# Neighbourhood attention by pairs of heads, with products alternating between halves of the systolic array

## The chip, the cores and the metric

The kernel runs on one NeuronCore of a Trainium2 chip as a single launch. The metric is the device time of one execution in microseconds, lower is better. The engines are named as in the profile: PE (TensorE, matrix products; PEld is its weight load), DVE (VectorE), ACT (ScalarE), POOL (GpSimd) and SP (SyncE, which issues most DMAs). [...]

## What is computed

The reference is a two-layer backbone over 256 latent tokens and 256 context tokens of width 1024. The mixer of layer 0 joins neighbourhood attention (8 heads of dimension 64) with a Hyena operator. The change touches only that attention. Each latent query sees a window of the grid and all context keys in one softmax; context queries see the context keys.

```python
def neighbourhood_attention(q, k, v, k_ctx, v_ctx, rpb):
    ...
        s_win = jnp.einsum('bhqd,bhrqjd->bhqrj', q_r, k_w).astype(jnp.float32) * scale + bias
        s_ctx = jnp.einsum('bhqd,bhcd->bhqc', q_r, k_ctx).astype(jnp.float32) * scale
        s = jnp.concatenate([s_win.reshape(b, h, GRID_W, n_win), s_ctx], axis=-1)
        p = jax.nn.softmax(s, axis=-1).astype(v.dtype)
        p_win = p[..., :n_win].reshape(b, h, GRID_W, wr, WIN_C)
        return (jnp.einsum('bhqrj,bhrqjd->bhqd', p_win, v_w)
                + jnp.einsum('bhqc,bhcd->bhqd', p[..., n_win:], v_ctx))

def dense_attention(q, k, v):
    s = jnp.einsum('bhqd,bhkd->bhqk', q, k).astype(jnp.float32) * (q.shape[-1] ** -0.5)
    p = jax.nn.softmax(s, axis=-1).astype(v.dtype)
    return jnp.einsum('bhqk,bhkd->bhqd', p, v)

# layer 0: na_hyena_mixer
    a_lat = merge_heads(neighbourhood_attention(qk_norm(qa_l, q_gain), qk_norm(ka_l, k_gain), va_l,
                                                k_c, va_c, rpb))
    b_lat = hyena_operator(p_lat[..., 3 * NA_WIDTH:], conv_w, conv_b, filter_params, d_bias)
    o_lat = jnp.concatenate([a_lat, b_lat], axis=-1) @ w_out
    ...
    a_ctx = merge_heads(dense_attention(qk_norm(qa_c, q_gain), k_c, va_c))
```

## The kernel before

All activations lie feature-major in SBUF: 128 features on the partitions, 512 tokens (256 latent, 256 context) along the free axis. Most products keep float32 accuracy by splitting each operand into a high and a low part (names ending in hi and lo) and taking three products hi·hi, lo·hi, hi·lo. The program's order is written out by hand: each engine's queue has its instructions in the order in which the Python code emits them. A tile of the PSUM pool psp (seven banks) or of the page pool in SBUF is reused once its last reader is done.

The attention (mixer0, line 911) runs beside the Hyena projections in a loop of 12 steps. Step i first makes one projection tile: in_tile (line 563), 24 products of 512 columns into the tile pi. It fetches its weight with w_get, which also splits a later weight tile (ACT writes whi, DVE writes wlo, line 153) and, in its place, issues the DMA of another from SP. Then attend(i) (line 1075) does one step of the attention: the values of head i-2, the transposes of head i-1, and the scores of head i. After it come the two halves of a Hyena convolution (conv; DVE lines 918 and 920; tiles x1c in even steps, vc in odd ones), with the head's exponentials (exps, on ACT) between them and its normalising (norm, on DVE) behind them. In some steps the transposes pzt of a Hyena block (z_trans) follow.

For one head, the pieces are:

- scores (line 992): queries and keys of two heads share a tile pair, head 2b on partitions 0 to 63 and head 2b+1 on partitions 64 to 127. A product has a 64-row contraction. psc holds the scores of 128 latent queries against all 512 keys (two tiles per head), pscc those of 2 x 128 context queries against 256 context keys. DVE then takes maxima (lines 1013 to 1019), adding the position bias, a tile loaded per head by load_bias from SP.
- exps and norm: ACT exponentiates into pr and prc and sums into sm; DVE inverts sm (line 1033) and scales pr and prc (lines 1035, 1037).
- transposes (line 1042): 12 PE transposes into ptp and ptc, copied to pt and ptc in SBUF by ACT and DVE (line 1051).
- values (line 1063): six products with a 64-column result into one half of the partitions of pao, in plain float32, which PE runs as two passes each. When both heads of a pair are done, cat_put splits pao into chi and clo (line 181).

The inner loop of the score products, which the change rewrites, is

```python
            def mm(o, q0, k0):
                for n, (a, b) in enumerate(((q, k), (q, kl), (ql, k))):
                    T.matmul(o, lhsT=a[r, q0:q0 + P], rhs=b[r, k0:], start=n == 0, stop=n == 2)
```

where r is the head's half of the partitions. In the opening stage of the kernel (mods, line 789) there are products of another small shape: their results have 32 rows, and successive products go to the four groups of 32 partitions of the tile pmod in turn.

Of the kernel before, what the change touches and what calls it, by code (L numbers as in the profile page):

```python
# [30 lines left out]
# columns of the packed per-partition constants  # L31
# [18 lines left out]
def _mod_tiles():  # L50
    """(layer, index, feature block) of the modulation VectorE makes, in order."""
    return [(l, i, b) for l, i in [(0, j) for j in range(2, 9)] + [(1, j) for j in range(9)] for b in range(KB)]


def body(ctx, tc, I, out):
# [38 lines left out]
    # ---------------------------------------------------------------- constants  # L94
# [11 lines left out]
    # ---------------------------------------------------------------- weights  # L106
# [52 lines left out]
    def w_halves():  # L159
        """The next tile's split in two steps; nothing is loaded in its place."""  # L160
# [22 lines left out]
    def w_paged():  # L183
        """The next tile, split into pages: for where whl's buffers are all in use."""
# [27 lines left out]
    # ---------------------------------------------------------------- modulation  # L212
# [37 lines left out]
    # ---------------------------------------------------------------- residual and norms  # L250
# [8 lines left out]
    def sumsq(s, m, late=None):  # L259
        """Adds block m's squares; the addition itself is left to the caller where a list is given."""  # L260
# [16 lines left out]
    def rsqrt_steps(y, src, scale, n):  # L277
        """y (SBUF) = (src*scale + eps)^-1/2, src in PSUM; one VectorE operation between yields."""
# [25 lines left out]
    def norm_h(s, k, l, n, dst):  # L304
        """dst: (hi, lo) APs of block k, stream s. Returns what is left to do once hi is there."""
# [25 lines left out]
    # H: list of KB (hi, lo), each [P, 512] = lat | ctx  # L331
# [15 lines left out]
    class Norm:  # L347
        """Norm n of layer l, whose sums of squares are complete per stream in turn."""
# [117 lines left out]
    def first_group(norm, mid=None):  # L466
        """The first 4 feature tiles after a norm; the latents go first, the context's norm runs beside."""
# [102 lines left out]
    # ---------------------------------------------------------------- SwiGLU  # L570
# [62 lines left out]
    def parted(a, j):  # L633
        """a[j] becomes its two parts."""
# [79 lines left out]
    def decay_scalars():  # L714
        """Decay exponents: log_sigmoid of the logits."""
# [20 lines left out]
    def start():  # L736
# [78 lines left out]
        def normed(s, m):  # L815
            """Blocks 2m and 2m+1 of stream s, normed."""
# [93 lines left out]
    # ---------------------------------------------------------------- layer 0 mixer  # L910
    def mixer0(norm_in, norm_out):
# [62 lines left out]
        # attention  # L974
# [9 lines left out]
        def qk_split(b):  # L984
            """Queries and keys of heads 2b and 2b + 1 in two parts each."""
# [6 lines left out]
        def scores(h):  # L992
            r = slice(64 * (h % 2), 64 * (h % 2) + 64)
            (q, ql), (k, kl) = qks[h // 2]
            bi = bias.pop(h)

            def mm(o, q0, k0):
                for n, (a, b) in enumerate(((q, k), (q, kl), (ql, k))):
                    T.matmul(o, lhsT=a[r, q0:q0 + P], rhs=b[r, k0:], start=n == 0, stop=n == 2)
# [3 lines left out]
            for qb in range(2):  # L1003
                mm(pl[qb], qb * P, 0)
# [546 lines left out]
```

## Time and profile before

| | |
|---|---|
| median of 3 timed runs | 1912.69 us (1911.32 to 1914.88) |
| the profiled execution, its span | 1918.3 us |
| PE busy | 1894.8 us (99%) |
| DVE busy | 1210.1 us (63%) |
| ACT busy | 701.5 us (37%) |
| POOL busy | 65.6 us (3%) |
| mean granted TensorE clock | 0.994 of full speed |

The profiled execution is one run recorded by the hardware profiler; its span reaches from the first to the last instruction. [...] A release shown in brackets names what ended an idle time.

### The profile page before, as it was taken

The numbers are of one execution on the slowest core, as the hardware profiler recorded it, in microseconds if no ns is written. First come the engines' busy times: TensorE is split into PE (matmuls) and PEld (weight loads), VectorE is DVE, ScalarE is ACT, GpSimd is POOL, SyncE is SP. The second block draws the span as 40 slices with busy tenths as digits, with TensorE's granted clock in tenths as the row PEclk, the third lists the DMA queues.
The fourth block names the chain that finished last, engine by engine and source line by source line (L and its number), as shares of the span: only waits on it lengthen the run. The fifth ranks groups of instructions, "written<-read, shape, count | busy, mean of one in ns | idle before, by whom it ended". The sixth has DMA issues, their size and how long they took to land.

```text
span 1918.3 us, 26355 instructions
## 1 busy us (share of the span) xinstructions
PE 1894.8 (99%) x10646; PEld 1627.5 (85%) x10646; DVE 1210.1 (63%) x1870; ACT 701.5 (37%) x1085; POOL 65.6 (3%) x73
## 2 busy tenths in 40 slices
PE   8999999999999999999999999999999999999999
PEld 5788888798877798878887988888889999999999
DVE  5577677777676776676766655433346755567554
ACT  4332122245554352222222422122233544465442
POOL 1010000002001200000000000000000200000000
PEclk9999999999999999999999999999999999999999
DMA  9355445532323235554555256423323432355653
GB/s 355 117 175 197 150 165 183 200 95 82 99 66 92 77 108 166 174 197 144 185 193 169 85 190 209 142 88 94 116 82 99 133 100 88 100 178 184 197 181 129
DMA packets 77899, 277.52 MB, mean 145 GB/s; under 512 B 8657, under 2 KB 9681, under 8 KB 77650
## 3 DMA queue, kind: packets, MB, share of 16 engines
q1 hardware_dynamic: 76626, 273.76, 43.2%
q0 software_dynamic: 1152, 2.10, 0.4%
q8 instruction: 83, 1.36, 0.3%
q14 instruction: 38, 0.31, 0.0%
HBM read 274.77 MB, written 1.05 MB: 144 GB/s over the span
## 4 chain that ended last, share of the span: by engine, by line
PE 87%; DMA 5%; DVE 5%; issue 1%; ACT 1%; SPq 0%; POOL 0%; DVEq 0%; POOLq 0%; ACTq 0%
PE pi L208 13%; PE pi L209 13%; PE pi L210 13%; PE po L209 9%; PE po L208 9%; PE po L210 9%; DMA wm<-in_wmt_dram 5%; DVE wlo L153 2%; PE fg L208 2%; PE fg L210 2%; PE fg L209 2%; PE pv L1297 2%; PE pv L1296 2%; PE pv L1295 2%; DVE junk L237 1%
## 5 line engine op out<-in xcount | busy, mean ns | idle before, releaser
L208 PE MATMUL pi<-hhi,whi 128*128 128x512 f32 (+1 forms) x1488 | 545.9, 367 | 0.0
L210 PE MATMUL pi<-hhi,wlo 128*128 128x512 f32 (+1 forms) x1488 | 545.2, 366 | 0.0
L209 PE MATMUL pi<-hlo,whi 128*128 128x512 f32 (+1 forms) x1488 | 545.2, 366 | 0.0
L153 DVE TENSOR_TENSOR wlo<-raw,whi 128x1024 fp32r<-128x1024 f32 (+1 forms) x325 | 421.8, 1314 | 165.5 <-ACT whi L89 164.9
L89 ACT ACTIVATE whi<-raw 128x1024 fp32r<-128x1024 f32 (+1 forms) x329 | 363.9, 1115 | 394.0 <-PE po L209 161.5
L237 DVE CUSTOM_DVE_ANT_0 junk<-wm,scb,cst 128x1024 bf16<-128x1024 f32 x224 | 291.1, 1299 | 97.0 <-DMA wm<-in_wmt_dram 93.2
L208 PEld LDWEIGHTS pi<-hhi,whi 128*128 128x128 f32 x1488 | 279.8, 188 | 52.2 <-issue 1.1
L210 PEld LDWEIGHTS pi<-hhi,wlo 128*128 128x128 f32 x1488 | 279.6, 188 | 49.5
L209 PEld LDWEIGHTS pi<-hlo,whi 128*128 128x128 f32 x1488 | 279.6, 188 | 49.2
L208 PE MATMUL po<-ghi,whi 128*128 128x512 f32 (+1 forms) x770 | 271.1, 352 | 6.9 <-ACT ghi L89 6.9
L209 PE MATMUL po<-glo,whi 128*128 128x512 f32 (+1 forms) x770 | 270.2, 351 | 0.2 <-DVE glo L181 0.2
L210 PE MATMUL po<-ghi,wlo 128*128 128x512 f32 (+1 forms) x770 | 270.1, 351 | 0.0
L89 ACT ACTIVATE ghi<-sg 128x512 fp32r<-128x512 f32 (+1 forms) x88 | 50.9, 579 | 396.7 <-DVE sg L580 393.5
L208 PEld LDWEIGHTS po<-ghi,whi 128*128 128x128 f32 x770 | 145.7, 189 | 29.1 <-ACT ghi L89 8.2
L209 PEld LDWEIGHTS po<-glo,whi 128*128 128x128 f32 x770 | 145.8, 189 | 22.4 <-DVE glo L181 1.5
L210 PEld LDWEIGHTS po<-ghi,wlo 128*128 128x128 f32 x770 | 145.7, 189 | 20.4
L391 DVE SCALAR_TENSOR_TENSOR x<-po,gate,x 128x256 f32<-128x256 f32 x136 | 61.3, 480 | 126.2 <-PE po L210 125.9
L580 DVE TENSOR_TENSOR sg<-sg,pi 128x512 f32<-128x512 f32 (+1 forms) x79 | 49.1, 622 | 100.3 <-PE pi L210 99.1
L181 DVE TENSOR_TENSOR glo<-sg,ghi 128x512 fp32r<-128x512 f32 (+1 forms) x88 | 55.1, 626 | 56.9 <-ACT ghi L89 56.9
L89 ACT ACTIVATE sq<-x 128x256 f32<-128x256 f32 (+1 forms) x71 | 30.1, 439 | 120.3 <-DVE x L391 120.2
L1297 PE MATMUL pv<-whi,hlo 128*128 128x256 f32 x256 | 72.1, 282 | 0.0
L1295 PE MATMUL pv<-whi,hhi 128*128 128x256 f32 x256 | 72.1, 282 | 0.0
(331 smaller groups left out, 2438.7 us busy)
## 6 DMA issues: line engine op xcount, KB each, us to landing
raw<-in_ffi_dram SPq DMA_DIRECT2D x176, 512.0 KB, 3.7
wm<-in_wmt_dram SPq DMA_DIRECT2D x128, 512.0 KB, 4.5
raw<-in_ffo_dram SPq DMA_DIRECT2D x64, 704.0 KB, 4.8
raw<-in_rt_dram SPq DMA_DIRECT2D x64, 512.0 KB, 3.7
raw<-in_ev_dram SPq DMA_DIRECT2D x32, 512.0 KB, 3.6
wm<-in_wm_dram SPq DMA_DIRECT2D x32, 256.0 KB, 5.7
x<-in_xt_dram SPq DMA_DIRECT2D x8, 256.0 KB, 5.4
bias<-in_rpb_dram SPq DMA_DIRECT2D x8, 256.0 KB, 4.2
```

The source lines that it names most:

```text
L89: S.activation(out=out, in_=in_, func=func, **k)
L153: V.tensor_tensor(out=lo[:, :n], in0=t[:, :n], in1=f(hi[:, :n]), op=ALU.subtract)
L181: V.tensor_tensor(out=lo, in0=src, in1=f(hi), op=ALU.subtract)
L208: T.matmul(o, lhsT=w[0][:, c0:c1], rhs=x[0][:, x0:x1], start=start, stop=False)
L209: T.matmul(o, lhsT=w[0][:, c0:c1], rhs=x[1][:, x0:x1], start=False, stop=False)
L210: T.matmul(o, lhsT=w[1][:, c0:c1], rhs=x[0][:, x0:x1], start=False, stop=stop)
L237: V.tensor_tensor_reduce(out=junk, in0=t, in1=scb[:, s, :], scale=1.0, scalar=bcol, op0=ALU.mult, op1=ALU.add, accum_out=MOD[l][:, idx, b, ...
L391: V.scalar_tensor_tensor(out=xs(s, m), in0=p[:, c0:c0 + L], scalar=gate[:, m, s:s + 1], in1=xs(s, m), op0=ALU.mult, op1=ALU.add)
L580: V.tensor_tensor(out=sg, in0=sg, in1=pb[:, :w], op=ALU.mult)
L1295: T.matmul(po[tb], lhsT=H[k][0][:, hs_], rhs=w[0][:, ws_], start=k == 0, stop=False)
L1296: T.matmul(po[tb], lhsT=H[k][0][:, hs_], rhs=w[1][:, ws_], start=False, stop=False)
L1297: T.matmul(po[tb], lhsT=H[k][1][:, hs_], rhs=w[0][:, ws_], start=False, stop=k == KB - 1)
```

## The change

The attention works on two heads at a time. pair_mm emits the three products of head 2b and of head 2b+1 in turn, so that each product uses the other half of the array's rows (partitions 0 to 63, 64 to 127) than the one before it and writes another PSUM tile. scores is split in two: scores_lat does the latent queries of both heads (four psc tiles) in even steps, scores_ctx the context queries of both (two pscc tiles) in odd steps. Each has its own exps and norm, which run in the same step. The transposes of both heads stand together in the next even step, and the values of both in the odd step after, where the products of the two heads alternate between the two halves of pao's partitions, that is of the array's columns. Two bias tiles are loaded at a time, at the end of the odd steps. The number of products, exponentials, maxima over scores and transposes is unchanged; some small operations on mx and sm are joined. The diff also removes comments throughout, which is left out here.

```diff
-        def scores(h):
-            r = slice(64 * (h % 2), 64 * (h % 2) + 64)
-            (q, ql), (k, kl) = qks[h // 2]
...
+        def pair_mm(b, o, q0, k0):
+
+            (q, ql), (k, kl) = qks[b]
+            for n, (x, y) in enumerate(((q, k), (q, kl), (ql, k))):
+                for j in range(2):
+                    r = slice(64 * j, 64 * j + 64)
+                    T.matmul(o[j], lhsT=x[r, q0:q0 + P], rhs=y[r, k0:], start=n == 0, stop=n == 2)
+
+        def scores_lat(b):
+
+            bi = [bias.pop(2 * b + j) for j in range(2)]
+            pl = [[ps(name="psc") for _ in range(2)] for _ in range(2)]
             for qb in range(2):
-                mm(pl[qb], qb * P, 0)
...
+                pair_mm(b, pl[qb], qb * P, 0)
+            prs = [[page(name="pr") for _ in range(2)] for _ in range(2)]
...
+            each = [(qb, j, 2 * qb + j) for qb in range(2) for j in range(2)]
+            for qb, j, i in each:
+                V.tensor_reduce(out=mx[:, 4 + i:5 + i], in_=pl[qb][j][:, L:], axis=AX.X, op=ALU.max)
...
+            def exps():
+                for qb, j, i in each:
+                    act(prs[j][qb][:, :L], prs[j][qb][:, :L], AF.Exp, bias=mx[:, 4 + i:5 + i],
+                        accum_out=sm[:, i:i + 1])
...
+        def scores_ctx(b):
+
+            pc = [ps([P, 2, 256], name="pscc") for _ in range(2)]
             for qb in range(2):
...
+                pair_mm(b, [p[:, qb, :] for p in pc], L + qb * P, L)
...
+        def values(b, turned):
+
+            po = pso.tile([P, 512], F32, tag="po", name="pao")
             for kb in range(4):
...
+                for j in range(2):
+                    T.matmul(po[64 * j:64 * j + 64, :L], lhsT=vt[kb][:, (2 * b + j) * 64:(2 * b + j + 1) * 64],
+                             rhs=turned[j][0][kb // 2][:, kb % 2, :], start=kb == 0, stop=kb == 3)
...
         def attend(i):
...
+            b, odd = divmod(i, 2)
+            if odd and b - 1 in turned:
+                values(b - 1, turned.pop(b - 1))
+            if not odd and b - 1 in lat:
+                prs, prc = lat.pop(b - 1)[0], con.pop(b - 1)[0]
+                turned[b - 1] = [transposes(prs[j], prc[j]) for j in range(2)]
+            if b < 4 and not odd:
+                lat[b] = scores_lat(b)
+                left.append(lat[b][1:])
+            if b < 4 and odd:
+                con[b] = scores_ctx(b)
+                left.append(con[b][1:])
+                for a in qks.pop(b):
                     drop(*a)
...
+                for j in range(2):
+                    load_bias(2 * b + 2 + j)
+                if b < 3:
+                    qk_split(b + 1)
...
             if i < 8:
+                ex, nor = left.pop(0)
                 c = z_conv(i // 2, p, i % 2 == 0)
                 next(c)
-                scored[i][2]()
+                ex()
                 next(c, None)
-                scored[i][3]()
+                nor()
```

On PE, in step 0, the score products of the first head stood as follows before (the numbers tell tiles of one name apart; psc_3931 and psc_3932 are the two query blocks of head 0, and all six products use array rows 0 to 63):

```order
L999 MATMUL psc_3931<-qkhi_3886,qkhi_3882 128x512
L999 MATMUL psc_3931<-qklo_3887,qkhi_3882 128x512
L999 MATMUL psc_3931<-qkhi_3886,qklo_3883 128x512
L999 MATMUL psc_3932<-qkhi_3886,qkhi_3882 128x512
L999 MATMUL psc_3932<-qklo_3887,qkhi_3882 128x512
L999 MATMUL psc_3932<-qkhi_3886,qklo_3883 128x512
```

On PE, in step 0 after the change (psc_3931 is head 0, psc_3932 head 1, for the first query block; psc_3933 and psc_3934 begin the second):

```order
L998 MATMUL psc_3931<-qkhi_3886,qkhi_3882 128x512
L998 MATMUL psc_3932<-qkhi_3886,qkhi_3882 128x512
L998 MATMUL psc_3931<-qklo_3887,qkhi_3882 128x512
L998 MATMUL psc_3932<-qklo_3887,qkhi_3882 128x512
L998 MATMUL psc_3931<-qkhi_3886,qklo_3883 128x512
L998 MATMUL psc_3932<-qkhi_3886,qklo_3883 128x512
L998 MATMUL psc_3933<-qkhi_3886,qkhi_3882 128x512
L998 MATMUL psc_3934<-qkhi_3886,qkhi_3882 128x512
```

The second head's products moved up between those of the first, and the context products (pscc) moved from here to the next step.

On PE, the values of head 0 in step 2 before (pt and ptc are the transposed weights of the head, vt the values):

```order
L1066 MATMUL pao_4113<-pt_4005,vt_3874 64x256
L1066 MATMUL pao_4113<-pt_4005,vt_3876 64x256
L1066 MATMUL pao_4113<-pt_4006,vt_3878 64x256
L1066 MATMUL pao_4113<-pt_4006,vt_3880 64x256
L1069 MATMUL pao_4113<-ptc_4026,vt_3878 64x256
L1069 MATMUL pao_4113<-ptc_4026,vt_3880 64x256
```

On PE, the values of heads 0 and 1 in step 3 after the change (pt_4089, pt_4090 and ptc_4110 belong to head 0; pt_4112, pt_4113 and ptc_4133 to head 1):

```order
L1085 MATMUL pao_4228<-pt_4089,vt_3874 64x256
L1085 MATMUL pao_4228<-pt_4112,vt_3874 64x256
L1085 MATMUL pao_4228<-pt_4089,vt_3876 64x256
L1085 MATMUL pao_4228<-pt_4112,vt_3876 64x256
L1085 MATMUL pao_4228<-pt_4090,vt_3878 64x256
L1085 MATMUL pao_4228<-pt_4113,vt_3878 64x256
L1085 MATMUL pao_4228<-pt_4090,vt_3880 64x256
L1085 MATMUL pao_4228<-pt_4113,vt_3880 64x256
L1089 MATMUL pao_4228<-ptc_4110,vt_3878 64x256
L1089 MATMUL pao_4228<-ptc_4133,vt_3878 64x256
```

The values of the first head moved from step 2 to step 3 and alternate there with those of the second.

On DVE, behind the maxima of head 0's psc in step 0, before:

```order
L1017 TENSOR_SCALAR mx<-mx 128x2
L1018 TENSOR_REDUCE mx<-pscc 128x2
L1019 TENSOR_SCALAR mx<-mx 128x2
L918 SCALAR_TENSOR_TENSOR x1c<-pi,cst,x1c 128x2x255
L920 SCALAR_TENSOR_TENSOR x1c<-pi,cst,x1c 128x2x255
L1032 TENSOR_TENSOR sm<-sm 128x2
L1033 RECIPROCAL sm<-sm 128x4
L1035 TENSOR_SCALAR pr<-pr,sm 128x512 x2
L1037 TENSOR_SCALAR prc<-prc,sm 128x256 x2
L153 TENSOR_TENSOR wlo<-raw,whi 128x1024
L1051 COPY pt<-ptp 128x2x128 x2
```

On DVE, from the reciprocal of step 0 to the end of step 1's context part, after the change:

```order
L1027 RECIPROCAL sm<-sm 128x4
L1029 TENSOR_SCALAR pr<-pr,sm 128x512 x4
L153 TENSOR_TENSOR wlo<-raw,whi 128x1024
L1043 TENSOR_REDUCE mx<-pscc 128x2 x2
L1044 TENSOR_SCALAR mx<-mx 128x4
L181 TENSOR_TENSOR qklo<-qy,qkhi 128x512 x2
L918 SCALAR_TENSOR_TENSOR vc<-pi,cst,vc 128x2x255
L920 SCALAR_TENSOR_TENSOR vc<-pi,cst,vc 128x2x255
L954 TENSOR_TENSOR x1c<-x1c,vc 128x512
L1052 RECIPROCAL sm<-sm 128x4
L1054 TENSOR_SCALAR prc<-prc,sm 128x256 x4
L153 TENSOR_TENSOR wlo<-raw,whi 128x1024
```

The context maxima moved behind the normalising of four pr tiles and a weight split, and the normalising of prc to the end of the odd step.

## Rows read from the trace of the kernel before

**Rows 1.** The page: span; busy time by engine; the chain that ended last.

```profile
span 1918.3 us, 26355 instructions
...
PE 1894.8 (99%) x10646; PEld 1627.5 (85%) x10646; DVE 1210.1 (63%) x1870; ACT 701.5 (37%) x1085; POOL 65.6 (3%) x73
...
PE 87%; DMA 5%; DVE 5%; issue 1%; ACT 1%; SPq 0%; POOL 0%; DVEq 0%; POOLq 0%; ACTq 0%
```

**Rows 2.** The chain in order of time: start us, length us, work.

```profile
509.75 1.59 PE psc L999 x6
...
534.66 1.59 PE psc L999 x6
...
604.62 0.86 PE pao L1069 x4
```

**Rows 3.** Timeline of PE, head 0: start us, us, instruction, count.

```profile
500.32 0.49 PE L999 MATMUL psc<-qkhi 64*128 64x512 f32 x1
500.65 0.39 PE L999 MATMUL psc<-qklo,qkhi 64*128 64x512 f32 x1
...
501.82 0.28 PE L999 MATMUL pscc<-qkhi 64*128 64x256 f32 x1
...
502.40 0.28 PE L999 MATMUL pscc<-qkhi,qklo 64*128 64x256 f32 x1
502.61 0.50 PE L208 MATMUL pi<-hhi,whi 128*128 128x512 f32 x1
502.95 0.39 PE L209 MATMUL pi<-hlo,whi 128*128 128x512 f32 x1
...
508.28 1.03 PE L1047 MATMUL ptp<-cst,pr 128*128 128x128 f32 x8
...
509.68 0.50 PE L999 MATMUL psc<-qkhi 64*128 64x512 f32 x1
```

**Rows 4.** The same timeline, around the values of head 0.

```profile
517.42 0.40 PE L210 MATMUL pi<-hhi,wlo 128*128 128x512 f32 x1
517.74 1.94 PE L1066 MATMUL pao<-pt,vt 128*64 128x256 f32 x8
519.52 1.03 PE L1069 MATMUL pao<-ptc,vt 128*64 128x256 f32 x4
```

**Rows 5.** Timeline of PE in the opening stage, the products of pmod.

```profile
20.70 3.64 PE L793 MATMUL pmod<-wm,c 128*32 128x512 f32 x32
```

**Rows 6.** Timeline of DVE, steps 2 and 3; in brackets idle time before, and releaser.

```profile
522.94 0.42 DVE L1013 TENSOR_REDUCE mx<-psc 128x1 f32<-128x256 f32 x1 [0.49 <-PE psc L999]
...
524.79 0.17 DVE L1017 TENSOR_SCALAR mx<-mx 128x2 f32<-128x2 f32 x1
...
525.67 0.74 DVE L918 SCALAR_TENSOR_TENSOR x1c<-pi,cst,x1c 128x510 f32<-128x510 f32 x1
...
527.11 0.15 DVE L1032 TENSOR_TENSOR sm<-sm 128x2 f32<-128x2 f32 x1
527.94 0.18 DVE L1033 RECIPROCAL sm<-sm 128x4 f32<-128x4 f32 x1 [0.68 <-ACT prc L89]
...
529.56 1.23 DVE L153 TENSOR_TENSOR wlo<-raw,whi 128x1024 fp32r<-128x1024 f32 x1
534.24 0.86 DVE L1051 COPY pt<-ptp 128x256 f32<-128x256 f32 x2 [3.46 <-ACT pt L89]
535.59 0.42 DVE L1013 TENSOR_REDUCE mx<-psc 128x1 f32<-128x256 f32 x1 [0.49 <-PE psc L999]
...
544.08 1.22 DVE L153 TENSOR_TENSOR wlo<-raw,whi 128x1024 fp32r<-128x1024 f32 x1
```

**Rows 7.** Timeline of ACT, step 2: the first exponential, and what follows the last.

```profile
525.00 0.51 ACT L89 ACTIVATE pr<-pr,mx 128x256 f32<-128x256 f32 x1 [1.68 <-DVE mx L1017]
...
527.80 0.78 ACT L89 ACTIVATE zT<-pzt 128x128 f32<-128x128 f32 x4
```

**Rows 8.** The page, DMA issues: tile, queue, count, KB each, median us to landing.

```profile
bias<-in_rpb_dram SPq DMA_DIRECT2D x8, 256.0 KB, 4.2
```

More of the change, by code (lines that the diff above doesn't have):

```diff
@@ L990, in qk_split @@
                 drop(qk[w][b])
-        def scores(h):
-            r = slice(64 * (h % 2), 64 * (h % 2) + 64)
-            (q, ql), (k, kl) = qks[h // 2]
[L995 to L999, printed above, removed]
-            load_bias(h + 1)
-            pl = [ps(name="psc") for _ in range(2)]
-            for qb in range(2):
-                mm(pl[qb], qb * P, 0)
-            pc = ps([P, 2, 256], name="pscc")
-            for qb in range(2):
-                mm(pc[:, qb, :], L + qb * P, L)
-            prs = [page(name="pr") for _ in range(2)]
-            prc = page([P, 2, 256], name="prc")
+        def pair_mm(b, o, q0, k0):
[4 more added lines that the diff above has]
+                    T.matmul(o[j], lhsT=x[r, q0:q0 + P], rhs=y[r, k0:], start=n == 0, stop=n == 2)
@@ new lines, in scores_lat @@
+            return prs, exps, norm
+        def scores_ctx(b):
+            pc = [ps([P, 2, 256], name="pscc") for _ in range(2)]
+            for qb in range(2):
+                pair_mm(b, [p[:, qb, :] for p in pc], L + qb * P, L)
+            prc = [page([P, 2, 256], name="prc") for _ in range(2)]
+            mx = sml.tile([P, 8], F32, tag="mx", name="mx")
+            sm = sml.tile([P, 8], F32, tag="sm", name="sm")
+            for j in range(2):
+                V.tensor_reduce(out=mx[:, 2 * j:2 * j + 2], in_=pc[j], axis=AX.X, op=ALU.max)
+            V.tensor_scalar(out=mx[:, 4:8], in0=mx[:, 0:4], scalar1=-1.0, scalar2=None, op0=ALU.mult)
+            def exps():
+                for i in range(4):
+                    act(prc[i // 2][:, i % 2, :], pc[i // 2][:, i % 2, :], AF.Exp, bias=mx[:, 4 + i:5 + i],
+                        accum_out=sm[:, i:i + 1])
@@ L1040, in scores @@
-            return prs, prc, exps, norm
+                for i in range(4):
+                    V.tensor_scalar(out=prc[i // 2][:, i % 2, :], in0=prc[i // 2][:, i % 2, :],
+                                    scalar1=sm[:, i:i + 1], scalar2=None, op0=ALU.mult)
+            return prc, exps, norm
         def transposes(prs, prc):
@@ L1068, in values @@
             for kb in range(2):
-                T.matmul(po[r, L:], lhsT=vt[2 + kb][:, h * 64:(h + 1) * 64], rhs=ptc[:, kb, :],
-                         start=kb == 0, stop=kb == 1)
-            drop(*pt, ptc)
-        scored, turned, po = {}, {}, {}
-        def attend(i):
-            if 0 <= i - 2 < 8:
-                h = i - 2
-                if h % 2 == 0:
-                    po[0] = pso.tile([P, 512], F32, tag="po", name="pao")
-                values(h, *turned.pop(h), po[0])
-            if 0 <= i - 1 < 8:
-                turned[i - 1] = transposes(*scored.pop(i - 1)[:2])
-            if i < 8:
-                scored[i] = scores(i)
-            if 0 <= i - 2 < 8 and i % 2:
-                cat_put((i - 2) // 2, po[0])
-            if i < 8 and i % 2:
-                for a in qks.pop(i // 2):
+                for j in range(2):
+                    T.matmul(po[64 * j:64 * j + 64, L:], lhsT=vt[2 + kb][:, (2 * b + j) * 64:(2 * b + j + 1) * 64],
+                             rhs=turned[j][1][:, kb, :], start=kb == 0, stop=kb == 1)
@@ new lines, in values @@
+            for pt, ptc in turned:
+                drop(*pt, ptc)
+            cat_put(b, po)
+        lat, con, turned = {}, {}, {}
+        left = []
+        def attend(i):
+            b, odd = divmod(i, 2)
[11 more added lines that the diff above has]
+                for a in qks.pop(b):
```

42 lines of the change are left out of this document (15 added, 27 removed).

## Prediction

> **What bounds the kernel now.** I read the page first. TensorE (PE) is busy for 99% of the 1918.3 us span and 87% of the chain that ended last is its products [rows 1]. So time is gained where PE issues fewer column-cycles or waits less, and nowhere else. Next I read the chain in order of time through the attention: in each step there is PE, and hardly anything else, from the first scores at 500.3 us to the last values at 605.5 us, with one pair of heads taking 534.66 - 509.75 = 24.9 us [rows 2, 3]. The reader should see that nothing waits here now: VectorE (DVE) and ScalarE (ACT) have slack. Then I read PE's own timeline. Since products are pipelined, the distance between starts counts, not the printed duration. Score products of a latent query block (psc, 512 columns, 64 of 128 rows of the array) start 1.17/5 = 0.234 us apart; those of a context block (pscc, 256 columns) 0.58/5 = 0.116 us apart [rows 3]. Value products (pao, 64 of 128 columns of the array, float32, two passes each) start 1.78/8 = 0.2225 us apart per pass [rows 4]. In each of them half of the array is idle.
>
> **A: scores.** There are 48 psc and 48 pscc products (6 + 6 for each of 8 heads): 48 x 0.234 + 48 x 0.116 = 16.8 us. After the change the products of heads 2b and 2b+1 stand in turn, on array rows 0-63 and 64-127, each head into its own PSUM bank. If two halves run side by side, the cost is halved: 8.4 us gone. No row of this trace has two row halves next to each other, so the bounds are: nothing overlaps (0), or worse, each change of half costs a gap as a change of shape does now (a rival, below); or full overlap (8.4). Between them, weight loads could take turns, since each product has its own load [rows 1]: a load and a pscc product now fit in 0.116 us, so two loads need at most 0.232 us, which a psc pair has and a pscc pair has not; then pscc gains nothing and A is 5.6. I take 8.4, because the nearest row, the next one, shows halves of the other kind overlapping.
>
> **B: values.** 96 passes x 0.2225 = 21.4 us. They will alternate between array columns 0-63 and 64-127. Here the trace has a precedent: pmod in the opening stage, float32 products that alternate over four groups of 32 columns. Its 32 passes of 512 columns take 3.64 us [rows 5]; at pao's rate they would take 32 x 0.445 = 14.2 us one after the other. Four groups thus ran nearly four times as fast. So two should run twice as fast: 10.7 us gone.
>
> [...]
>
> **C: changes of shape.** Going from full-array products to pao takes 0.32 us instead of 0.23, and out of psc/pscc 0.21 instead of 0.116, the next one 0.34 instead of 0.23 [rows 3, 4]: about 0.1 to 0.2 on each side of a block. Eight blocks of values become four; the eight blocks of scores stay eight. Four blocks less at 0.2 to 0.25 are 0.9 us. As a cross-check, PE's work for a pair afterwards: two projections 2 x 5.67 (502.61 to 508.28), transposes of two heads 2 x 1.4 (508.28 to 509.68) less one change of shape, 2.7, psc 1.5 + 0.1, the Hyena transposes 0.4, values 2.74 + 0.1, pscc 1.0; that is 19.9 us against 24.9, 5.0 per pair, and 4 x 5.0 = 20.0 = A + B + C.
>
> **D: what comes late instead.** DVE's work hardly shrinks. An even step runs from 522.94 to 529.56 with 0.68 idle, an odd one without a pause from 535.59 to 544.08; each then has a wlo (1.2) and two copies (0.8) [rows 6]. That is 7.9 + 10.5 = 18.4 us per pair, less some 0.4 for small operations that are merged: 18.0. A new wait is added: all four psc blocks come before the first exponential, so DVE reaches the sum sm while ACT still has eight exponentials to do, at (527.80 - 525.00)/6 = 0.47 us each [rows 7], 3.7 us, with only the two convolution steps (525.67 to 527.1) beside them. DVE stands idle about 2.6 us, and behind sm in its queue stand the normalising of pr, the weights' wlo, and the context maxima. DVE's round is thus 18.0 + 2.6 = 20.6 us against PE's 19.9.
>
> The first round is worse, as step 1 has no values yet. Counting from the first psc: the first maximum at 1.0, four groups at 0.93 each (1.85 for two, 522.94 to 524.79 [rows 6]) to 4.7, exponentials and sum to 8.9, pr and wlo to 11.9. The odd step's queue then gives pscc's normalised prc: 8.49 less the two psc groups, clo, pr and small things (3.6), plus a second pscc maximum (0.7): 5.6 us, so 17.5. PE gets there (pscc at 7.4, projection until 13.9, eight transposes) at 15.0 and waits 2.5 us at ptc. The next psc needs PSUM banks that DVE's first copy frees at 19.6, another 0.5. So the second pair's scores start at about 19.6 instead of 21.6 us: 2.0 of 5.0 gained, D1 = 3.0. The two later rounds lose 20.6 - 19.9 = 0.7 each. D = 4.4. Its bounds are 2.5 (only the first wait) and 8.8 (a first-round wait of 2.9 in both later rounds too).
>
> Work that moves at no cost: each pair's two bias loads stand on SP's queue after the odd step's weight load, which waits for that step's wlo at about 12 us of a round. They land 4.2 us later [rows 8] and are read at 20. The cover is some 4 us; without it DVE's first biased maximum, and PE behind it, would wait for the rest. The split of the next queries and keys, the convolutions and cat_put keep their steps. Everything after step 9 stands in its old order and moves up as a block.
>
> **Sum.** A 8.4 + B 10.7 + C 0.9 - D 4.4 = 15.6 us. The profiled execution, 1918.3 us, would be 1902.7. The timed runs have a median of 1912.7, 5.6 us below that span, so the prediction for them is 1897.0 us, 0.8% faster. About 0.2% (3.8 us) is what a measurement of this kernel can tell from no change.
>
> **Rivals.**
>
> 1. Row halves do not overlap, column halves do. For it: no row shows row halves side by side. Against it: pmod. A is 0; PE's round becomes 22.0, DVE's lag shrinks and only about 1.6 of D remains: 10.7 + 0.9 - 1.6 = 10.0, time 1902.7.
>
> 2. DVE and ACT become the bound of each round. For it: 20.6 against 19.9 on paper, and DVE already works 18 of 24.9 us. Against it: after the first round values stand between psc and pscc and give back 2.8 us. With the upper D, 8.8: 20.0 - 8.8 = 11.2, time 1901.5. [...]
>
> 3. Slower: each change between row halves stops the array as a change of shape does. It sits in the score blocks: 96 products, 88 changes inside blocks. At 0.2 us (0.1 in and 0.1 for the next [rows 3, 4]) they add 17.6; B and C still give 11.6, D vanishes: 6.0 slower, 1918.7. It decides for slower from 0.13 us per change. Against it: in pmod groups change at every product with no such gap. [...]
>
> 4. Neither kind overlaps here, and the change does not do what it says. C gives 0.9 and the waits vanish behind the slower PE: 1911.8. Against it: pmod.
>
> **How the numbers follow.** Forecast 0.66; rival 1 0.11; rival 2 0.11; rival 3 0.05; rival 4 0.07. Forecast and rivals 1 and 2 are faster by more than 0.2%: 0.88. Rival 4 is within it: 0.07. Rival 3 is slower: 0.05. The forecast by itself runs from 1892.7 (D gone, 20.0 gained) to 1899.8 (pscc pairs bound by their loads, 2.8 less). The range goes on to rivals 1 and 2, with a little for the spread of runs: 1892 to 1904. Rivals 3 and 4, 0.12, are left out.
>
> **What would show it.** In the changed kernel's timeline six pairs of psc should start within about 1.5 us and 24 pao passes within about 2.7 us, the two of a pair starting almost together. If psc pairs keep 0.234 per product, rival 1; if gaps grow above 0.3, rival 3. PE should wait once for some 2.5 us at ptc behind DVE's prc in the second round, and under 1 us later; waits of 3 us in each round mean rival 2. The distance from the first psc to the end of the last values, 105 us now, should be about 89. I am wrong if the products gain and the end does not move, or if a wait appears after the attention.

## The result, and the profile after

The changed kernel took 1891.8 us (median of 4 runs, 1885.1 to 1892.7) against 1913.8 us for the kernel before (1911.3 to 1916.8): 22.0 us less, ratio 0.9885 (95% interval 0.9862 to 0.9907). A second measurement of the same program (e2) gave 1894.95 us, ratio 0.9894 (0.9879 to 0.9908). The prediction was 1897.0 us and 15.6 us less, in a range from 1892 to 1904. It was right in sign and in what happens inside the attention, but the gain is 6 us larger, and the first time lies 0.2 us under the range; the second lies in it.

The page of the profiled execution, to be read beside [rows 1]:

```profile
span 1883.3 us, 26318 instructions
...
PE 1862.5 (99%) x10646; PEld 1607.7 (85%) x10646; DVE 1206.5 (64%) x1858; ACT 701.3 (37%) x1085; POOL 65.6 (3%) x73
...
PE 84%; DVE 6%; DMA 6%; issue 2%; ACT 1%; SPq 0%; POOL 0%; DVEq 0%; POOLq 0%; ACTq 0%
```

PE still sets the end: the same number of its instructions, 32 us less of busy time. The two profiled executions lie 35.0 us apart, 13 more than the medians, so it is stages that are compared below. PE's timeline at the first scores, beside [rows 3] (columns: start us, us, instruction, form, count):

```profile
491.79 0.50 PE L998 MATMUL psc<-qkhi 64*128 64x512 f32 x2
492.13 0.40 PE L998 MATMUL psc<-qklo,qkhi 64*128 64x512 f32 x2
492.37 0.40 PE L998 MATMUL psc<-qkhi,qklo 64*128 64x512 f32 x2
...
493.39 0.50 PE L208 MATMUL pi<-hhi,whi 128*128 128x512 f32 x1
```

and at the first values and context scores, beside [rows 4]:

```profile
520.40 1.95 PE L1085 MATMUL pao<-pt,vt 128*64 128x256 f32 x16
522.18 1.03 PE L1089 MATMUL pao<-ptc,vt 128*64 128x256 f32 x8
523.14 0.39 PE L998 MATMUL pscc<-qkhi 64*128 64x256 f32 x2
523.37 0.28 PE L998 MATMUL pscc<-qklo,qkhi 64*128 64x256 f32 x2
523.48 0.28 PE L998 MATMUL pscc<-qkhi,qklo 64*128 64x256 f32 x2
```

A row with x2 is a pair, one product on each half, so six pairs of psc take 493.39 - 491.79 = 1.60 us, where twelve single products at 0.234 us would take 2.8. Pairs start 0.23 us apart (pscc 0.115), as single products did before; sixteen pao passes take the 1.95 us that eight took. PE waits in one place of the attention, where the prediction put it:

```profile
509.20 0.68 PE L1074 MATMUL ptc<-cst,prc 128*128 128x128 f32 x4 [2.48 <-DVE prc L1054]
509.67 1.91 PE L1064 MATMUL ptp<-cst,pr 128*128 128x128 f32 x8
511.38 1.06 PE L1074 MATMUL ptc<-cst,prc 128*128 128x128 f32 x4
512.37 0.79 PE L998 MATMUL psc<-qkhi 64*128 64x512 f32 x2
```

Behind the wait of 2.48 us eight ptp take 1.91 us, where the same eight take 1.03 elsewhere [rows 3]. The windows of that stretch tell why (columns: window, length, PE busy with its instructions in brackets, granted clock, DMA share, GB/s):

```profile
506.20:509.20 3.00, 0.53 (x5) 1.00 0.63 244
509.20:510.70 1.50, 1.50 (x9) 0.65 0.02 5
510.70:512.20 1.50, 1.50 (x9) 0.50 0.20 41
512.20:513.70 1.50, 1.50 (x10) 0.71 0.86 289
513.70:515.20 1.50, 1.50 (x12) 1.00 0.05 19
```

The granted clock was 1.00 in the window in which PE stood, 0.65 in the first 1.5 us behind it, 0.50 and 0.71 in the next two windows, and 1.00 again in the one from 513.70, some 4 us after PE resumed.

The attention is counted from the first psc to the first pz, a product of the next stage. That pz, before and after (the first psc of before is in [rows 3]):

```profile
611.10 0.40 PE L208 MATMUL pz<-fhi,dfthi 128*128 128x512 f32 x1
```

```profile
586.86 0.39 PE L208 MATMUL pz<-fhi,dfthi 128*128 128x512 f32 x1
```

So the attention now takes 95.07 us instead of 110.78: 15.7 us less, 0.1 from the predicted 15.6. The 6 us more were gained outside it, where both kernels run the same instructions. Most experiments below are about them. This table gives for each run that distance, the wait at ptc, and the time (a dash: one run only, not compared):

| run | attention, us | wait at ptc, us | median, us | ratio to before (95% interval) |
|---|---|---|---|---|
| e1 kernel before | 110.78 | none | 1914.3 | 0.9991 (0.9979 to 1.0002) |
| e2 changed kernel | 94.83 | 2.5 | 1894.95 | 0.9894 (0.9879 to 0.9908) |
| e3 both by head | 102.93 | 1.5 | 1901.95 | 0.9927 (0.9911 to 0.9944) |
| e4 qklo on POOL | 95.41 | 3.4 | 1895.98 | 0.9903 (0.9886 to 0.992) |
| e5 changed, old addresses behind | 95.20 | 2.4 | 1897.8 | 0.9913 (0.9894 to 0.9931) |
| e6 before, new addresses behind | 110.69 | none | 1911.5 | 0.9982 (0.9964 to 1.0) |
| e7 scores by head | 95.93 | 1.5 | 1892.4 | - |
| e8 values by head | 101.66 | 2.5 | 1908.8 | - |
| e9 splits moved | 91.82 | 1.4 | 1889.98 | 0.9869 (0.9852 to 0.9887) |
| e10 splits, keys, transposes moved | 90.97 | none (0.6 at psc) | 1890.62 | 0.9877 (0.9856 to 0.9898) |
| e11 before, loads left out | 110.78 | none | 1905.47 | 0.9951 (0.9935 to 0.9967) |
| e12 changed, loads left out | 93.64 | 2.5 | 1883.05 | 0.9835 (0.9819 to 0.985) |
| e13 as e12, 32 bytes higher | 93.79 | 2.4 | 1888.47 | 0.9859 (0.9832 to 0.9886) |
| e14 as e11, 32 bytes higher | 110.76 | none | 1902.89 | 0.993 (0.9906 to 0.9955) |

### The profile page after: what moved, and what is told of

Read it like the earlier page. It is cut to its first block, busy times and chain, and to the rows that moved or that the text cites. A ratio compares the mean times of both kernels' runs of the same rounds, so it can differ in the third digit from the quotient of the medians.

```text
span 1883.3 us, 26318 instructions
## 1 busy us (share of the span) xinstructions
PE 1862.5 (99%) x10646; PEld 1607.7 (85%) x10646; DVE 1206.5 (64%) x1858; ACT 701.3 (37%) x1085; POOL 65.6 (3%) x73
## 3 DMA queue, kind: packets, MB, share of 16 engines
HBM read 274.77 MB, written 1.05 MB: 146 GB/s over the span
## 4 chain that ended last, share of the span: by engine, by line
PE 84%; DVE 6%; DMA 6%; issue 2%; ACT 1%; SPq 0%; POOL 0%; DVEq 0%; POOLq 0%; ACTq 0%
PE pi L208 12%; PE pi L209 12%; PE pi L210 12%; PE po L209 9%; PE po L210 9%; PE po L208 9%; DMA wm<-in_wmt_dram 6%; DVE wlo L153 3%; PE fg L208 2%; PE fg L210 2%; PE fg L209 2%; PE pv L1322 2%; PE pv L1323 2%; PE pv L1324 2%; DVE junk L237 1%
## 5 line engine op out<-in xcount | busy, mean ns | idle before, releaser
L1323 PE MATMUL pv<-wlo,hhi 128*128 128x256 f32 x256 | 71.7, 280 | 0.0
```

What stands on the lines that cost most here:

```text
L1323: T.matmul(po[tb], lhsT=H[k][0][:, hs_], rhs=w[1][:, ws_], start=False, stop=False)
```

## Experiments

**The two kernels again (e1, e2), without an edit.**

> The program of before, unchanged, profiled and timed a second time, to see how much its stages outside the attention vary from one execution to another. In the first pair of traces the attention (first psc to first pz) was 110.8 us before and 95.1 us after, 15.7 us less, but the stages outside it, which the change does not touch, differed by another 19 us between the two profiled executions, and the medians by 22.0 us. Theory 1 (chance): what lies outside the attention differs from execution to execution, by PE's waits for the modulation loads (2.9 us at 360, 3.4 us at 823, 1.8 us at 1012 in the profile before); here those waits take other values, summing anywhere between 1 and 9 us, the attention stays at 110.8 within 0.3, and the ratio to before is 1.000 within 0.002. Theory 2 (the change shortens other stages too): the waits stand at the same places with the same length within 0.5 us.

> The changed program, profiled and timed a second time, beside the same runs of before. Theory 1 (chance): with more runs of both the gain comes down from 22.0 towards the attention's 15.7 us, a ratio of about 0.992 (0.990 to 0.993), and the waits for the modulation loads at the ends of the feed-forward stages come back in the trace (0 to 9 us in all). Theory 2 (other stages are shorter too): the ratio stays at 0.9885, and the stages outside the attention are again some 6 us shorter than in the second profile of before.

The attention repeats to 0.3 us and the gain stays near 20. The ratio of e2, 0.9894, lies between what its two theories asked for: the waits came back, and other stages are shorter too. The long stages behind the attention are 0.3 to 0.5 us shorter each in the changed kernel, and they repeat to 0.01 us where PE does not wait.

**The pair without alternation (e3).**

```diff
-            for qb in range(2):
-                pair_mm(b, pl[qb], qb * P, 0)
+            for j in range(2):
+                for qb in range(2):
+                    pair_mm(b, pl[qb], qb * P, 0, (j,))
...
-            for kb in range(4):
-                for j in range(2):
+            for j in range(2):
+                for kb in range(4):
```

Here pair_mm makes the products of the heads in its last argument alone; the context scores and the ptc part of the values are put in the same order.

> The changed program with its pairs and steps, but the products of head 2b all before those of head 2b+1, in the scores and in the values: only the order of the products inside a block is undone. If the gain is the halves running side by side (A 8.4 and B 10.7 us of my sum), psc starts 0.234 us apart and pao 0.2225 us per pass again, the attention goes back to about 109 us (110.8 less 0.9 for fewer changes of shape, with one product per block still overlapping at the border of the two heads), and the time is within 2 us of before. If it is the pairing that helps, with fewer changes of shape and other waits, the attention stays near 95 us.

The attention came out at 102.93, between the two cases (about 109 and 95): half the gain without any alternation in the program. Its timeline shows how, and e7 shows it again, so:

**Only the scores by head (e7), only the values by head (e8).**

e7 keeps the first half of that diff and e8 the second.

> The changed kernel, but within a pair the scores of one head all stand ahead of those of the other; the values still alternate. By the run in which both were put head by head (score blocks took 9 places instead of 6, 20 pao passes instead of 12), theory that TensorE starts products of the other half a few instructions early: 3 x 0.232 + 3 x 0.116 = 1.04 us more per pair, 4.2 in all, so 95.0 + 4.2 = 99.2 us from the first psc to the first pz, 98.0 if some of it lies in the wait at ptc. Rival, halves overlap only where the program alternates: 6 places more of each kind per pair, 2.1 us, 8.4 in all: 103.4.

> The changed kernel, but within a pair the values of one head all stand ahead of those of the other; the scores still alternate. Theory that products of the other half start early: 8 passes more of 0.2225 us per pair, 7.1 in all, less up to 2 of the later waits that a slower TensorE hides: 95.0 + 5 to 7 = 100.0 to 102.1 us from the first psc to the first pz. Rival, overlap only where the program alternates: 12 passes more per pair, 10.7 in all, less up to 2: 103.7 to 105.7.

PE's timeline in e7, the first scores (the rows do not tell the heads apart; of two starts that lie closer than the 0.234 us of single products [rows 3], one is read as the other head's):

```profile
495.41 0.50 PE L998 MATMUL psc<-qkhi 64*128 64x512 f32 x1
495.75 0.39 PE L998 MATMUL psc<-qklo,qkhi 64*128 64x512 f32 x1
495.99 0.39 PE L998 MATMUL psc<-qkhi,qklo 64*128 64x512 f32 x1
495.99 0.62 PE L998 MATMUL psc<-qkhi 64*128 64x512 f32 x2
496.33 0.51 PE L998 MATMUL psc<-qklo,qkhi 64*128 64x512 f32 x2
496.57 0.51 PE L998 MATMUL psc<-qkhi,qklo 64*128 64x512 f32 x2
496.80 0.39 PE L998 MATMUL psc<-qkhi 64*128 64x512 f32 x1
```

The program has six products of head 0 and then six of head 1. The trace has three of head 0, three pairs, and three of head 1: head 1's first block ran beside head 0's second, past three products that stand ahead of it in the program. In e8 the last four passes of head 0 ran beside four of head 1 (the first two start at 528.38 and 528.39), 20 places instead of 24 or 12. So in these runs PE did not keep the program's order between products on different halves.

e8 fell in its range (101.66): against the two profiles of the changed kernel the order of the values is worth 6.6 to 6.8 us. e7's 95.93 lies under its range of 98.0 to 99.2: the order of the scores is worth 0.9 to 1.1 us, not 4.2. Its products do take longer, nine places instead of six, but PE then reaches ptc later, waits 1.5 instead of 2.5 us, and the granted clock stays at 1.00 behind it, so that the first round (from one pair's first psc to the next pair's) takes 19.3 us instead of 20.6. The later two take 20.8 and 20.7 instead of 20.1 and 20.0, 0.7 more each.

**Work taken from DVE by POOL (e4).**

```diff
-                split_to(qk[w][b], *qks[b][w])
+                act(qks[b][w][0], qk[w][b], AF.Copy)
+                G.tensor_tensor(out=qks[b][w][1], in0=qk[w][b], in1=f(qks[b][w][0]), op=ALU.subtract)
```

> The changed program with the low parts of the next pair's queries and keys (two qklo subtractions of 0.6 us per pair) made by POOL, which is idle there, instead of DVE. My sum put DVE's round at 20.6 us against PE's 19.9, and 2.5 us of PE's wait at ptc in the first round on DVE's queue. If DVE's queue is what keeps the last microseconds, the wait at ptc falls from 2.5 to about 1.3 us, the wait for banks before the second psc by as much, and the attention gets 1.2 to 2 us shorter (93.1 to 93.9). If PE alone sets the later rounds and the wait has another cause, nothing changes beyond 0.3 us.

Neither case came: the wait at ptc grew to 3.4 us. DVE in the changed kernel, and DVE and POOL in e4:

```profile
501.01 1.67 DVE L1029 TENSOR_SCALAR pr<-pr,sm 128x512 f32<-128x512 f32 x4
502.60 1.22 DVE L153 TENSOR_TENSOR wlo<-raw,whi 128x1024 fp32r<-128x1024 f32 x1
```

```profile
504.93 2.72 DVE L1030 TENSOR_SCALAR pr<-pr,sm 128x512 f32<-128x512 f32 x4
507.57 2.32 DVE L153 TENSOR_TENSOR wlo<-raw,whi 128x1024 fp32r<-128x1024 f32 x1
```

```profile
506.04 2.77 POOL L990 TENSOR_TENSOR qklo<-qy,qkhi 128x512 fp32r<-128x512 f32 x2 [12.00 <-ACT qkhi L89]
```

While POOL subtracts, DVE's pr and wlo take 1.05 and 1.10 us longer: 2.15 lost for the 1.28 that were taken away, 0.9 net, which is the growth of the wait. Each of the two was lengthened by most of one POOL subtraction (2.77 us for two, 1.4 each); by what mechanism, the trace does not show.

**Where the 6 us come from: the waits that vary (e11, e12).** PE's waits for ghi at the ends of feed-forward stages differ from execution to execution (us in total, times, longest): the first row below is of the kernel before, the second of the changed kernel; in e8 they are 11.6. Behind them stands DVE, which waits in its queue for weights of the modulation (last row, e2):

```profile
PE po L208 <- ACT ghi L89: 6.9, 3, 3.0
```

```profile
PE po L208 <- ACT ghi L89: 1.1, 1, 1.1
```

```profile
DVE junk L237 <- DMA wm<-in_wmt_dram: 90.5, 36, 5.0
```

```diff
-        t = modp.tile([P, D], F32, tag="wm", name="wm")
-        SY.dma_start(out=t, in_=I["wmt"][n])
-        mtile[n] = t
+        if n < 2:
+            t = modp.tile([P, D], F32, tag="wm", name="wm")
+            SY.dma_start(out=t, in_=I["wmt"][n])
+            wmt.append(t)
+        mtile[n] = wmt[n % 2]
```

> The kernel before, which loads only the first two of the 128 tiles of the modulation's weights and uses them again for the other 126: their loads are left out, so its modulation is not the reference's. Addresses and instructions of the engines stay. Theory, TensorE's waits at the ends of the feed-forward stages (po behind ghi, 6.9 us in the first profile of the kernel before, 5.4 in the second) come from VectorE standing in a queue behind a modulation step whose load is late, and vary from execution to execution: they fall under 1.5 us, the time to 1903 to 1908, and the runs lie within 4 us of each other. Rival, they come from ScalarE's or VectorE's own work: they stay, and so does the time.

> The changed kernel with the same left out (126 of the 128 loads of the modulation's weights). Theory: with that part gone, what is left between the two kernels is the attention and the addresses: 15.8 + 3.0 = 18.8 us less than the kernel before with the same left out, plus or minus 1; the attention stays at 95.0. Rival, the change also touches these waits: a difference over 21.

The waits are gone in both, and with them the scatter: runs lie within 0.4 and 1.1 us. But the difference is 22.4 us, not 18.8. That is the rival's number (over 21), yet it stands in two kernels without the waits, so they do not explain the 6 us. With PE undisturbed, the two profiles can be set side by side. PE at the first psc, the first pz and the end, in e11 and then in e12:

```profile
494.29 0.49 PE L1002 MATMUL psc<-qkhi 64*128 64x512 f32 x1
...
605.07 0.40 PE L208 MATMUL pz<-fhi,dfthi 128*128 128x512 f32 x1
...
1900.46 0.28 PE L210 MATMUL po<-ghi,wlo 128*128 128x256 f32 x1
```

```profile
492.56 0.50 PE L1001 MATMUL psc<-qkhi 64*128 64x512 f32 x2
...
586.20 0.39 PE L208 MATMUL pz<-fhi,dfthi 128*128 128x512 f32 x1
...
1877.75 0.28 PE L210 MATMUL po<-ghi,wlo 128*128 128x256 f32 x1
```

So 1.73 us were gained ahead of the attention, 17.14 in it, and 1295.39 - 1291.55 = 3.84 behind it. The attention gains 17.1 and not 15.7 because in this execution the clock did not fall behind the same wait at ptc of 2.48 us (columns as above):

```profile
507.20:510.00 2.80, 0.32 (x4) 1.00 0.62 234
510.00:511.50 1.50, 1.50 (x14) 1.00 0.00 0
511.50:513.00 1.50, 1.50 (x13) 1.00 0.47 41
```

**Addresses (e5, e6).** The attention takes its page buffers in a new order, so later tiles lie in other buffers. For these two runs the buffers were renamed at the start, which leaves order, waits and reuse as they are (e5; the list of e6 is its inverse; the loop gives pg0 to pg57 ascending addresses, as before):

```diff
-    free = [f"pg{i}" for i in range(NPAGE)]
+    free = [f"pg{i}" for i in [0, 1, 2, 3, 4, 5, 6, 7, 8, 25, 10, 32, 12, 49, 14, 15, 37, 33, 18, 57, 20, 16, 26, 9, 24, 41, 43, 22, 28, 29, 30, 31, 17, 45, 34, 19, 36, 35, 48, 39, 40, 47, 21, 11, 44, 27, 46, 23, 38, 13, 50, 51, 52, 53, 42, 55, 56, 54]]
...
+    for i in range(NPAGE):
+        pagep.tile([P, TOK], F32, tag=f"pg{i}", name="hold")
```

> The changed kernel, with nothing altered but the SBUF addresses behind the 58 page buffers: they are renamed so that from the end of the attention on every product reads exactly the addresses that it reads in the kernel before. Order of work, waits and the order in which buffers are reused stay. In the four profiles of kernels with pairs the stages behind the attention are shorter than in the two of the kernel before, by the same few tenths each (121.17 against 121.52, 183.79 against 184.11, 65.62 against 66.03, 58.32 against 58.86, 93.03 against 93.51 us; about 3 us in all), though their instructions are the same. Theory, addresses: those stages go back to 121.52, 184.11, 66.03, 58.86, 93.51 to within 0.05 us, the attention stays at 95 to within 0.5, and the time rises by 3 us from the last one of the changed kernel (1895), plus or minus 2 for the stages ahead of the attention, whose addresses change too: 1898. Rival, something that the attention leaves behind: the stages stay at 121.17, 183.79, 65.62, 58.32, 93.03 and the time at 1895.

> The kernel before, with the 58 page buffers renamed so that from the end of the attention on every product reads exactly the addresses that it reads in the changed kernel. Theory, addresses: the stages behind the attention go to 121.17, 183.79, 65.62, 58.32, 93.03 us to within 0.05, the attention stays at 110.8 to within 0.5, and the time falls by about 3 us, plus or minus 2 for the stages ahead of the attention: ratio 0.9984. Rival: the stages stay at 121.52, 184.11, 66.03, 58.86, 93.51 and the ratio at 1.000.

The last 840 us, from a sum of squares ss to PE's last product, in the kernel before (e1):

```profile
1065.90 0.59 PE L296 MATMUL ss<-acc,cst 128*128 128x256 f32 x2
...
1909.00 0.28 PE L210 MATMUL po<-ghi,wlo 128*128 128x256 f32 x1
```

in the changed kernel (e2):

```profile
1047.99 0.59 PE L296 MATMUL ss<-acc,cst 128*128 128x256 f32 x2
...
1888.31 0.28 PE L210 MATMUL po<-ghi,wlo 128*128 128x256 f32 x1
```

and in the changed kernel with the old addresses (e5):

```profile
1050.81 0.59 PE L298 MATMUL ss<-acc,cst 128*128 128x256 f32 x2
...
1893.91 0.28 PE L212 MATMUL po<-ghi,wlo 128*128 128x256 f32 x1
```

| | old addresses | new addresses |
|---|---|---|
| kernel before | 843.10 (e1) | 840.33 (e6) |
| changed kernel | 843.10 (e5) | 840.32 (e2) |

The distance goes with the addresses to 0.01 us and not with the program. Nor does it go with the chip: e1 and e5 ran on two chips, e2 and e6 on the same two, and on a third e11 has 843.06 and e12 840.32. This shows the addresses as the cause of 2.8 of the 3.84 us behind the attention; the other 1.1 lie ahead of that ss, where waits for ghi cover them in e5 and e6. In time e5 lies 2.9 us above e2 and e6 2.8 below e1; they ran beside other executions of the kernel before, and by the ratios it is 3.6 and 1.7.

**A shift of 32 bytes (e13, e14).** Ahead of the attention the kernels' buffers have the same names and differ only in shifts of 32 to 96 bytes, since a few of them hold slightly longer tiles.

```diff
+    for i in range(9):
+        pagep.tile([P, TOK + 8 * (i == 8)], F32, tag=f"pg{i}", name="hold")
```

This makes pg8 32 bytes longer and so moves pg9 to pg57 up.

> The changed kernel as in the run with the modulation's weights kept (126 of their 128 loads left out), with every page buffer from pg9 on 32 bytes higher in SBUF and nothing else changed: 8635 of the 10518 products read a moving operand at an address 32 bytes higher. Ahead of the attention the two kernels run the same instructions and differ only in such shifts (of 32, 64 or 96 bytes for 1575 of the 2267 products), yet the first psc comes at 492.56 us in one and at 494.29 in the other. Theory, those shifts are what it costs: the first psc moves by 0.3 to 2 us from 492.56, to either side, the second of the long stages ahead of it (182.85 us) changes by over 0.1, and so do stages behind the attention. Rival, a shift that all buffers share does nothing: first psc at 492.56, 182.85, 121.17, 183.79 to within 0.05, and the time at 1883.05.

> The kernel before, likewise with the modulation's weights kept and every page buffer from pg9 on 32 bytes higher. Theory: the first psc moves from 494.29 us by 0.3 to 2, and the stages of 183.81, 121.52 and 184.11 us change by over 0.1 each. Rival: they stay to within 0.05, and the time at 1905.47.

The changed kernel lost 5.4 us by it, the kernel before gained 2.6; by the ratios, as they ran beside other executions of the kernel before, it is 4.6 and 4.0, and by the spans of the profiles 5.8 and 2.9. First psc, first pz and end of e13:

```profile
494.57 0.50 PE L1003 MATMUL psc<-qkhi 64*128 64x512 f32 x2
...
588.36 0.39 PE L210 MATMUL pz<-fhi,dfthi 128*128 128x512 f32 x1
...
1883.60 0.28 PE L212 MATMUL po<-ghi,wlo 128*128 128x256 f32 x1
```

| us | ahead of the attention | attention | behind |
|---|---|---|---|
| before (e11) | 494.29 | 110.78 | 1295.39 |
| before, shifted (e14) | 494.43 | 110.76 | 1292.37 |
| changed (e12) | 492.56 | 93.64 | 1291.55 |
| changed, shifted (e13) | 494.57 | 93.79 | 1295.24 |

The attention keeps its time to 0.15 us; everything else moves by up to 2.0 us ahead of it and 3.7 behind. In e14 the first psc moved by 0.14 us alone, not by the 0.3 or more that was expected; its gain lies behind the attention. The 1.73 us that the changed kernel was shorter ahead of the attention are within what 32 bytes do (2.0 in e13). That those very shifts make them is not shown: no run had the other kernel's layout from the start.

**Shortening the wait at ptc (e9, e10).** DVE waits 2.5 us for ScalarE's exponentials in each even step, and behind that wait stand weight splits that nobody needs soon. In the changed kernel:

```profile
500.60 0.16 DVE L1026 TENSOR_TENSOR sm<-sm 128x4 f32<-128x4 f32 x1 [2.52 <-ACT pr L89]
```

e9 moves both splits of a pair of steps ahead of that wait:

```diff
-            p = in_tile()
+            p = in_tile(ahead=3 if i > 7 else 1 if i % 2 else 2)
             attend(i)
             if i < 8:
+                if i % 2 == 0:
+                    while wpos["split"] <= wpos["get"] + 3:
+                        w_split()
```

e10 also puts qklo behind prc's normalising, and the ptp of both heads ahead of the ptc, with its buffers renamed so that behind the attention the addresses are those of the changed kernel.

> The changed kernel, but in the attention both weight splits of a pair of steps stand behind the even step's maxima (where VectorE waits 2.5 us for ScalarE's exponentials) instead of one ahead of the context maxima and one ahead of the copies of the transposes. Addresses stay as in the changed kernel. Theory: prc is ready 1.2 us earlier, the wait at ptc falls from 2.5 to 1.3 us, and the granted clock does not fall behind it (it did not behind the 1.5 us wait of the run with scores head by head), which gives back another 1.7; VectorE's round falls from about 20.1 to 18.9, so that TensorE's own 19.9 sets the later ones: from the first psc to the first pz 92 us instead of 95.0, ratio to the kernel before 0.988. Rival, the wait at ptc moves on to the copies or the weights' lo parts: 95 as now, ratio 0.9895.

> As the run before, and in the odd step the lo parts of the next queries and keys stand behind prc's normalisation, and the latent transposes of both heads stand ahead of those of the context. The page buffers are renamed so that behind the attention every address is that of the changed kernel. Theory: no wait is left at ptc, all four rounds take TensorE's own 19.9 us: 91 us from the first psc to the first pz, ratio 0.9875. Rival, what stands behind prc now holds up the next scores: a wait of about 1.3 us appears at psc and it stays at 92.

```profile
510.55 0.63 PE L1074 MATMUL ptc<-cst,prc 128*128 128x128 f32 x4 [1.35 <-DVE prc L1054]
511.01 1.04 PE L1064 MATMUL ptp<-cst,pr 128*128 128x128 f32 x8
```

In e9 (above) the wait is 1.35 us, the ptp behind it keep 1.04 us, the later rounds take 19.7 and 19.8 us, and the attention 91.82: as expected. In e10 PE has no wait at ptc and 0.58 us at the next psc, for DVE's copies; the attention takes 90.97. e9, with the addresses of the changed kernel behind the attention, is the fastest median of a complete kernel, 1889.98 us. Its gain over the changed kernel in time (2 to 5 us) is less sure than the 3.0 us of its attention.

## The prediction, step by step

- **A, B and C (8.4, 10.7, 0.9; right).** Pairs of psc start 0.23 us apart, pscc 0.115, pao passes two per 0.22. e10, less its wait of 0.6, saves 110.78 - 90.37 = 20.4 us in the attention where the three terms are 20.0. The bound for loads that take turns (pscc gains nothing) did not occur, nor did rival 1 or rival 3: the two halves of the rows overlapped fully, and a change of half cost nothing that shows: a pair of psc takes the 0.23 us that a single took [rows 3].
- **D (4.4; the total right, its parts not).** 20.4 - 15.7 = 4.7 us were lost. The wait at ptc is 2.48 where 2.5 was predicted. But the first round took 20.6 us (psc at 491.79 and 512.37) instead of 19.6, as the working left out the clock; in e12, where it did not fall, it took 19.3. The later two took 20.1 and 20.0, not 20.6: DVE's round is shorter than worked out, some 17.4 us of work beside the wait of 2.52 where 18.0 and 2.6 stood in the sum. The two errors cancel, which is luck. Rival 2 fell: no wait of its size returns in the later rounds. In a small way DVE does set them, as in the forecast: PE's own round, seen in e9 and e10, is 19.7 to 19.8 us, so DVE holds it by 0.3.
- **The bias loads and the splits** that were costed at nothing cost nothing: no wait for them appears.
- **"Everything after step 9 stands in its old order and moves up as a block" (wrong).** It kept its order but not its length. This sentence, and the silent assumption of the same ahead of the attention, is the step that failed. It put at nothing what lies outside the attention: the new order of buffers and their sizes shift nearly every operand, and the products took 3.84 us less behind the attention and 1.73 ahead of it (e12 against e11). Of this 2.8 us are shown to be the addresses (e5, e6), the rest is argued from the size of what 32 bytes do. 15.7 + 5.6 = 21.3 of the 22.0 us measured at first; the rest is within what the waits for ghi vary. A range for it was missing: the two shifts of 32 bytes gave +5.4 and -2.6 us.
- **The sum from one profiled execution** (1918.3 us, less 5.6 to the median) worked only by this constant. Profiled executions of one program differ by 8.6 us (1883.3 and 1891.9 for the changed kernel), through the waits for ghi (1.1 and 4.5 us) and what follows them, among other things.
- **The signs to look for.** Six psc pairs in 1.60 us (about 1.5 predicted), 24 pao passes in 523.14 - 520.40 = 2.74 (2.7), first psc to the last values 581.27 - 491.79 = 89.5 (about 89): all three held. "A wait after the attention" did not appear.

The gain of the change itself is thus the attention's, 15.7 to 17.1 us. Some 5.6 us of the measured 22 are, as far as is known, luck of the layout, which the next edit can take back: between the two shifted kernels the difference is 14.4 us.

## What to carry to other kernels

Products that use half of the array's rows or columns are worth pairing: both kinds ran twice as fast here (two psc in 0.23 us, where one took 0.234; two pao passes in 0.22, where one took 0.2225), and what to work out then is which engine's queue the shorter round runs into. A shift of 32 bytes made 0.24 and 0.21% here by the ratios, and 0.29% by the medians of e12 and e13. So in a kernel that PE bounds, as this one, a difference of 0.2 to 0.3% between two versions proves little about an edit as long as their buffers lie at other addresses; compare the stage that was edited in the trace, and take away waits that vary before reading the rest. Where one engine waits for another in the middle of its queue, put work there that is needed late, as e9 did: 3.0 us of its attention.

## What the runs showed of the hardware

- The rate of products changed with the addresses of their operands in SBUF: 32 bytes on most moving operands moved the whole program by +5.4 and -2.6 us with the same instructions. In the last feed-forward of the kernel before (the last 170 us, 1440 products of 256 columns) starts lie 112 to 128 ns apart, 118.2 in the mean. In the changed kernel, with other addresses, they lie 112 to 125 ns apart, 117.5 in the mean, and place by place the distances differ by up to 10 ns. With the addresses of the kernel before, the last 840 us of the changed kernel took the same 843.10 us (e5, e1). Which property of an address decides stays open.
- Products on the other half of the array started ahead of earlier ones: head by head, score blocks took 9 places instead of 12 (e3, e7), and values 20 instead of 24 (e8).
- Behind the pause at ptc (2.4 to 2.5 us) the granted clock fell to 0.50 for 3 to 4 us in the changed kernel, e2, e5 and e8; in e4 it fell late in the pause of 3.4 us (0.87 in the mean of 511.10 to 514.10, 0.50 in the next 1.5 us). It stayed at 1.00 in e12 and e13 behind pauses of the same 2.4 to 2.5 us. Behind pauses of 1.35 us (e9) and 1.5 us (e3, e7) it stayed at 1.00. In the first round that is 20.6 (changed kernel) against 19.3 us (e12).
- A subtraction on POOL lengthened DVE's operations beside it by 1.05 and 1.10 us (e4).
